# Decode step with paged indexer keys: pages loaded by register address and scored four at a time, without a gathered copy

## The chip, the cores and the metric

The kernel runs on one core of a Trainium2 chip. The metric is the device time of one execution in microseconds, and the figure shown for a kernel is the median of its timed runs. A separate execution is profiled; its trace is where all rows below come from. Names of engines: PE is the matrix engine (PEld its weight load), DVE the vector engine, ACT the scalar engine, POOL GpSimd, and SP the engine that here does nothing but issue DMAs. Each engine executes its own instructions strictly in order.

## The reference, cut to what matters

One layer of a hybrid decoder is computed for a prompt of 512 tokens and for 8 sample sequences of one token each. Both go through one projection, a gated DeltaNet in eight heads, a sparse attention, an output projection and a feed-forward of width 8192. The change touches only the sparse attention of the samples, and in it only the indexer: every sample scores all of its 4096 past keys and its own key, and keeps the best 256.

```python
def indexer_scores(q_i, w_i, k_i):
    s = jax.nn.relu(jnp.einsum("bqhd,bld->bqhl", q_i, k_i).astype(F32))
    return jnp.einsum("bqhl,bqh->bql", s, w_i.astype(F32)) * (D_IDX ** -0.5)
...
    ki_past = cache_kidx[page_table].reshape(B, past, D_IDX)
    ki_all = jnp.concatenate([ki_past.astype(k_i_new.dtype), k_i_new], axis=1)
...
    score = indexer_scores(q_i, w_i, ki_all)
    idx, valid = select_topk(score, q_pos, key_pos, n_sel)
```

There are 16 indexer heads of 128, and the past keys lie in pages of 128 keys x 128 numbers, 64 KB each in fp32. The page table names 32 pages for each of the 8 samples, so 256 pages, 16.8 MB, are read.

## The kernel before, in words

The whole layer is one stream of weight tiles through PE. All 520 tokens are the moving operand, in two halves of 260 columns; a weight tile of 128 output columns is loaded from memory in two pieces of 512 KB (line 363, tile `wr`), split by ACT and DVE into a high and a low part (lines 327 and 328), and multiplied in three products for each of 16 blocks of rows and each half (lines 446 to 448, tile `acc`). The order of the weight tiles is written out by hand (`ORDER`): indexer queries `qi0` to `qi15`, then heads of `k` and `z`, the shared keys and values, and so on. From `qi15` on, an operation of the modulation (`ada_op`, line 481) follows each tile; it takes two more pieces of 512 KB and issues four fp32 matmuls of 32 output rows by 512 columns, each on its own quarter of the array's columns (`tile_position=(0, 32*g)`).

Everything that is not this stream is a Python generator (a job) that is advanced by one step at every tick; a tick falls after each quarter of a tile and half. So the order of instructions on each engine is fixed when the kernel is built: a job's yields say how much of the stream stands between its steps. `topk` (lines 814 to 833) starts its prompt selection on POOL with three `affine_select` (line 823), which come ten ticks after `qi15`, and goes on on DVE (lines 829 and 830). `conv` (line 1295 and on) needs POOL as well (line 1302).

The sample scores are made in two steps. `gather_pages` copies all pages into a scratch tensor `kscr` in the order of the page table: 16 rounds of two halves, each an indirect DMA of 512 KB into a tile `gst` (line 856) and a plain DMA from there to `kscr` (line 858), all issued by POOL. A round is let go by a small copy of a finished accumulator (`pace`, lines 788 and 851), so that the rounds lie along the stream of `qi` tiles. `scores`, ten ticks after `qi15`, then loads four pages of one sample with one DMA of 256 KB from `kscr` (line 877, tile `pg`, issued by SP, the queue that loads the weights too), one load for each tick; up to three loads later it multiplies them by the sample's 32 query columns (two samples share a quarter of the array; line 868). So the 64 products of 32 rows x 512 columns come one at a time, each with a tick's worth of the stream between it and the next. After the eight products of a block `c` the result is rectified and reduced over the heads (lines 887 to 897). Eight blocks make the 4096 keys.

Tiles come from shared sets of buffers: `b` (24 buffers of 2 KB per partition: page tiles, convolution tiles, head tiles), `d` (4 buffers, `gst` among them), `s` (11 small ones), and four `wr` buffers. A load into a buffer waits on SP until the last reader of the buffer is done.

Of the kernel before, what the change touches and what calls it, by code (L numbers as in the profile page):

```python
# [9 lines left out]
F32 = mybir.dt.float32  # L10
F32R = mybir.dt.float32r
I32 = mybir.dt.int32
AF = mybir.ActivationFunctionType
OP = mybir.AluOpType
# [14 lines left out]
PAST = 4096  # L29
NPG = PAST // 128  # L30
# [26 lines left out]
G0 = 6  # L57
TK = (1, 2, 2)
RXB = 5
TD = 3  # L60
SY = 2
SW = 10
RXL = 4
# [174 lines left out]
class Kern:  # L238
# [541 lines left out]
    def qidx(self, j, accs):  # L780
        nc = self.nc
        if j == NE:
            self.bias_rows()
        qh, ql = self.B("qih", [128, NT], F32R), self.B("qil", [128, NT], F32R)
        self.evac(qh, accs)
        if self.pacing:
            self.pace = self.tiny.tile([128, 1], F32, name="pace0")
            nc.scalar.copy(self.pace, accs[0][:, 0:1])
        for h in range(2):
            s = slice(h * HF, (h + 1) * HF)  # L790
            nc.vector.tensor_tensor(ql[:, s], accs[h], qh[:, s].bitcast(F32), op=OP.subtract)  # L791
        for s in range(2):
            o = SEQ + 4 * s - HF
            nc.scalar.copy(self.QI[:, 4 * s:4 * s + 4, 16 * s + j], accs[1][:, o:o + 4])
        yield 2
        for i in range(1, NQ):
            w = 128 * (i + 1)
            qs = slice(128 * i, w)
            ps = self.m()
            nc.tensor.matmul(ps[:, :w], qh[:, qs], self.kih[:, :w], start=True, stop=False)  # L800
            nc.tensor.matmul(ps[:, :w], qh[:, qs], self.kil[:, :w], start=False, stop=False)
            nc.tensor.matmul(ps[:, :w], ql[:, qs], self.kih[:, :w], start=False, stop=True)
            rl = self.B("rl", [128, 512])
            nc.scalar.activation(rl[:, :w], ps[:, :w], AF.Relu)
            sc = self.sc[i]
            wcol = self.wq[:, i, j:j + 1]
            if j == 0:
                nc.vector.tensor_scalar(sc, rl[:, :w], wcol, None, op0=OP.mult)
            else:
                nc.vector.scalar_tensor_tensor(sc, rl[:, :w], wcol, sc, op0=OP.mult, op1=OP.add)  # L810
            yield 1
# [21 lines left out]
            nc.vector.tensor_scalar(self.sc[i], self.sc[i], mark, -1.0, op0=OP.is_equal, op1=OP.add)  # L833
        self.masks = True

    def gather_pages(self):

        nc, I = self.nc, self.I
        self.kscr = self.dr.tile([256, 16, 1024], F32, name="kscr")
        rows = I["ckt"].rearrange("a (g d) s -> (a g) (d s)", d=8)  # L840
        pg = self.S("pgi", [128, 2], I32)
        nc.scalar.dma_start(pg, I["pt"].rearrange("o (h p) -> p (o h)", p=128))
        ix = self.S("pgx", [128, 2, 16], I32)
        nc.gpsimd.iota(ix, pattern=[[0, 2], [1, 16]], base=0, channel_multiplier=0)
        nc.gpsimd.tensor_scalar(pg, pg, 16.0, None, op0=OP.mult)
        nc.gpsimd.tensor_tensor(ix, ix, pg[:, :, None].to_broadcast([128, 2, 16]), op=OP.add)
        for g in range(16):
            while self.pace is None:
                yield 1

            mark = nc.gpsimd.tensor_copy(self.tiny.tile([128, 1], F32, name="pace"), self.pace)
            self.pace = None
            with self.tc.issue_after(mark.ins):
                for hf in range(2):
                    t = self.L("gst", [128, 1024])
                    nc.gpsimd.indirect_dma_start(out=t, out_offset=None, in_=rows,
                                                 in_offset=bass.IndirectOffsetOnAxis(ap=ix[:, hf, g:g + 1], axis=0))
                    nc.gpsimd.dma_start(self.kscr[hf * 128:(hf + 1) * 128, g], t)
        self.pacing = False

    def scores(self):

        nc = self.nc
        todo = []

        def product():
            sp, b4, s, pg = todo.pop(0)
            nc.tensor.matmul(sp[32 * b4:32 * b4 + 32, :], self.QI[:, 4 * s + b4, :], pg.rearrange("p a b -> p (a b)"),  # L868
                             start=(s == 0), stop=(s == 1), tile_position=(0, 32 * b4))

        for c in range(PAST // 512):
            sp = None
            for b4 in range(4):
                for s in range(2):
                    pg = self.B("pg", [128, 4, 128])
                    n = (4 * s + b4) * NPG + c * 4
                    nc.sync.dma_start(pg, self.kscr[n:n + 4].rearrange("t g (d s) -> (g d) t s", s=128))
                    sp = sp or self.m()
                    todo.append((sp, b4, s, pg))
                    yield 1  # L880
                    if len(todo) > TD:
                        product()
            while todo:
                yield 1
                product()
            rl = self.B("rls", [128, 512])
            nc.scalar.activation(rl, sp, AF.Relu)
            yield 1
            ps = self.m()
            for hf in range(2):  # L890
                o = 128 - (2 * c + hf)
                nc.tensor.matmul(ps[:, 0:256], self.bs[:, o:o + 128], rl[:, hf * 256:(hf + 1) * 256],
                                 start=(hf == 0), stop=(hf == 1))
            if c == 0:
                nc.scalar.copy(self.SC[:, 0:256], ps[:, 0:256])
            else:
                nc.vector.tensor_tensor(self.SC[:, 0:256], self.SC[:, 0:256], ps[:, 0:256], op=OP.add)

        p2 = self.m()
        for b4 in range(4):  # L900
            for s in range(2):
                b = 4 * s + b4
                nc.tensor.matmul(p2[32 * b4:32 * b4 + 32, 0:1], self.QI[:, b, :], self.ki[:, SEQ + b:SEQ + b + 1],
                                 start=(s == 0), stop=(s == 1), tile_position=(0, 32 * b4))
        rn = self.S("rn", [128, 1])
        nc.scalar.activation(rn, p2[:, 0:1], AF.Relu)
        yield 2
        p2 = self.m()
        nc.tensor.matmul(p2[:, 8:9], self.bs[:, 113:241], rn, start=True, stop=True)
        nc.vector.tensor_tensor(self.SC[:, 256:257], p2[:, 8:9], self.c("cm"), op=OP.add)  # L910
        self.spawn(self.select())
# [342 lines left out]
    def stage_in(self):  # L1254
        nc, I, kp = self.nc, self.I, self.kp
# [30 lines left out]
        self.qb, self.nl, self.nkeys, self.natt = {}, {}, 0, 0  # L1286
        self.zdone, self.odone, self.sdone, self.wdone = set(), set(), set(), set()
        self.masks = self.attending = False
        self.pace, self.pacing = None, True
        self.nqb = 0  # L1290

    def conv(self, name, h, accs):
# [402 lines left out]

    def proj(self, name):
        accs = self.stream(self.x1)
        if self.pacing and not name.startswith("qi"):
            self.pace = self.tiny.tile([128, 1], F32, name="pace0")
            self.nc.scalar.copy(self.pace, accs[0][:, 0:1])  # L1700
        self.post(name, accs)

    def post(self, name, accs):
# [22 lines left out]
            self.gate(h, accs, getattr(self, "mx", None))  # L1726

    def open_in(self):
        self.kn = self.S("kn", [128, 2])
        self.rel = self.S("rel", [32, 8]), self.L("oh", [32, 640])  # L1730
        for t, n in ((self.kn, "kn"), (self.rel[0], "rel"), (self.rel[1], "oh")):
            self.nc.scalar.dma_start(t, self.I[n])
        self.stage_in()
        self.spawn(self.gather_pages())

    def open_mix(self):

# [543 lines left out]
```

## Time and profile before

| | |
|---|---|
| median of 3 timed runs | 2928.33 us (2926.22 to 2936.08) |
| the profiled execution | 2940.01 us |
| its span, first to last instruction | 2938.3 us |
| mean granted clock of PE | 0.966 of full speed |
| instructions | 55405 |
| moved by DMA | 499.64 MB, of which 37.76 MB on the queue that POOL feeds |

The span is what the rows below divide; 1.7 us of the profiled execution lie outside it.

### The profile page before, as it was taken

Reading aid. Unit: us, or ns where it says so; the run is one execution under the profiler, and the core shown is the slowest. Engines: PE = TensorE matmul, PEld = TensorE weight load, DVE = VectorE, ACT = ScalarE, POOL = GpSimd, SP = SyncE. Lnnn points to the kernel's source line nnn. Section 1 sums busy time; section 2 is a strip of 40 time slices with the busy share of each in tenths; the row PEclk is TensorE's granted clock in tenths of the full one; section 3 lists DMA queues with packets and bytes.
Section 4 is the critical chain, followed back from the end, with each engine's and each line's share of the span. In section 5 each row is a group of like instructions: output and inputs, shape, how many; then the busy total and the mean of one; then the engine's idle time right before and its main releaser. Section 6 shows DMA issues by size and latency. Waiting matters only on the chain.

```text
span 2938.3 us, 55405 instructions
## 1 busy us (share of the span) xinstructions
PE 2736.5 (93%) x21584; PEld 2508.4 (85%) x21584; DVE 1731.0 (59%) x3367; ACT 1573.6 (54%) x2796; POOL 1133.8 (39%) x961
## 2 busy tenths in 40 slices
PE   6999969999998998999988999999999898998996
PEld 3689856778897887888987999999999898898996
DVE  4464264338576555632786555555566666776767
ACT  3234222223544443333565777777778676676863
POOL 0012221112212333211463665565675556545513
PEclk9999989999999999999998999999999999999998
DMA  7868766754443555567665434334343333332354
GB/s 259 284 225 260 251 222 192 218 166 156 154 153 123 186 162 179 193 238 261 222 202 160 144 123 141 130 127 141 126 153 131 108 121 125 109 108 102 116 174 158
DMA packets 201533, 499.64 MB, mean 170 GB/s; under 512 B 23832, under 2 KB 74392, under 8 KB 201272
## 3 DMA queue, kind: packets, MB, share of 16 engines
q1 hardware_dynamic: 162544, 421.81, 43.1%
q10 hardware_dynamic: 27464, 36.53, 4.1%
q0 software_dynamic: 11264, 37.76, 3.6%
q8 instruction: 170, 2.79, 0.4%
q14 instruction: 91, 0.75, 0.1%
HBM read 430.34 MB, written 65.68 MB: 169 GB/s over the span
## 4 chain that ended last, share of the span: by engine, by line
PE 63%; DVE 10%; DMA 10%; ACT 6%; issue 5%; POOL 5%; another core or an unknown queue 0%; ACTq 0%; SPq 0%; POOLq 0%; DVEq 0%
PE acc L446 18%; PE acc L447 17%; PE acc L448 17%; DMA gst<-in_ckt,pgx 4%; ACT wh L431 3%; DVE wl L437 3%; POOL S L374 3%; PE m L868 2%; PE m L481 2%; ACT stg L436 2%; DMA kscr<-gst 2%; DVE xf L328 1%; PE m L590 1%; DMA wr<-in_win 1%; PE m L275 1%
## 5 line engine op out<-in xcount | busy, mean ns | idle before, releaser
L437 DVE TENSOR_TENSOR wl<-stg,wh 128x512 fp32r<-128x512 f32 (+1 forms) x584 | 489.7, 866 | 377.3 <-ACT wh L431 318.8
L446 PE MATMUL acc<-hh,wh 128*128 128x260 f32 (+1 forms) x1984 | 591.6, 300 | 11.7 <-DVE qil L791 6.0
L448 PE MATMUL acc<-hh,wl 128*128 128x260 f32 (+1 forms) x1984 | 567.0, 287 | 12.3 <-DVE wl L328 12.2
L447 PE MATMUL acc<-hl,wh 128*128 128x260 f32 (+1 forms) x1984 | 569.5, 287 | 0.6 <-DVE hl L623 0.6
L446 PE MATMUL acc<-xf,wh 128*128 128x260 f32 x1824 | 525.9, 288 | 42.2 <-DVE f L2164 21.9
L448 PE MATMUL acc<-xf,wl 128*128 128x260 f32 x1824 | 524.1, 287 | 6.7 <-DVE wl L328 4.8
L328 DVE TENSOR_TENSOR wl<-wr,wh 128x512 fp32r<-128x512 f32 (+1 forms) x478 | 352.1, 751 | 295.9 <-ACT wh L327 292.0
L447 PE MATMUL acc<-xf,wh 128*128 128x260 f32 x1824 | 523.3, 287 | 0.0
L327 ACT CAST wh<-wr 128x512 fp32r<-128x512 f32 (+1 forms) x478 | 284.3, 612 | 437.1 <-PE acc L447 193.9
L446 PEld LDWEIGHTS acc<-hh,wh 128*128 128x128 f32 (+1 forms) x1984 | 376.7, 190 | 113.0 <-issue 80.8
L374 POOL TENSOR_TENSOR S<-wr,wr 128x1024 f32<-128x1024 f32 x112 | 274.8, 2454 | 329.9 <-DMA wr<-in_wff 257.2
L446 PEld LDWEIGHTS acc<-xf,wh 128*128 128x128 f32 x1824 | 352.0, 193 | 45.5 <-ACT wh L431 19.2
L448 PEld LDWEIGHTS acc<-hh,wl 128*128 128x128 f32 (+1 forms) x1984 | 377.3, 190 | 14.4 <-DVE wl L328 12.6
L447 PEld LDWEIGHTS acc<-hl,wh 128*128 128x128 f32 (+1 forms) x1984 | 377.8, 190 | 8.4 <-DVE hl L623 4.8
L448 PEld LDWEIGHTS acc<-xf,wl 128*128 128x128 f32 x1824 | 352.0, 193 | 8.1 <-DVE wl L328 5.0
L447 PEld LDWEIGHTS acc<-xf,wh 128*128 128x128 f32 x1824 | 351.9, 193 | 0.0
L436 ACT COPY stg<-S 128x512 f32<-128x512 f32 (+1 forms) x334 | 241.7, 732 | 105.5 <-DVE wl L437 81.8
L448 PE MATMUL acc<-h2h,wl 128*128 128x260 f32 x928 | 266.5, 287 | 8.5 <-DVE wl L328 8.5
L446 PE MATMUL acc<-h2h,wh 128*128 128x260 f32 x928 | 266.1, 287 | 7.5 <-ACT h2h L327 5.2
L447 PE MATMUL acc<-h2l,wh 128*128 128x260 f32 x928 | 266.5, 287 | 4.5 <-DVE h2l L328 4.5
L446 PE MATMUL acc<-T,wh 128*128 128x260 f32 x896 | 256.4, 286 | 8.0 <-DVE fr L2020 3.0
L448 PE MATMUL acc<-T,wl 128*128 128x260 f32 x896 | 256.5, 286 | 2.0 <-DVE wl L328 2.0
(545 smaller groups left out, 5882.4 us busy)
## 6 DMA issues: line engine op xcount, KB each, us to landing
wr<-in_wff SPq DMA_DIRECT2D x256, 512.0 KB
wd<-in_wada SPq DMA_DIRECT2D x106, 512.0 KB
wr<-in_win SPq DMA_DIRECT2D x106, 512.0 KB
wr<-in_wada SPq DMA_DIRECT2D x86, 512.0 KB
wr<-in_wout SPq DMA_DIRECT2D x48, 512.0 KB
st<-f SPq DMA_DIRECT2D x32, 520.0 KB
kscr<-gst POOLq DMA_DIRECT2D x32, 512.0 KB
pg<-kscr SPq DMA_DIRECT2D x64, 256.0 KB
```

The source lines that it names most:

```text
L275: self.nc.tensor.transpose(out, in_, self.ident[:n, :n])
L327: self.nc.scalar.copy(hh, x)
L328: self.nc.vector.tensor_sub(hl, x, hh.bitcast(F32))
L374: self.nc.gpsimd.tensor_tensor(t, a, b, op=op)
L431: nc.scalar.copy(hh, x)
L436: nc.scalar.copy(p, x[:, s])
L437: nc.vector.tensor_tensor(hl[:, s], p, hh[:, s].bitcast(F32), op=OP.subtract)
L446: T.matmul(acc, wh[:, cs], xh, start=first, stop=False, skip_group_check=goes_on)
L447: T.matmul(acc, wh[:, cs], xl, start=False, stop=False, skip_group_check=goes_on)
L448: T.matmul(acc, wl[:, cs], xh, start=False, stop=last, skip_group_check=goes_on)
L481: self.nc.tensor.matmul(self.aacc[v][32 * g:32 * g + 32, :], self.cs[:, kt, :], w[:, j * 512:(j + 1) * 512], start=(kt == 0), stop=(kt == ...
L868: nc.tensor.matmul(sp[32 * b4:32 * b4 + 32, :], self.QI[:, 4 * s + b4, :], pg.rearrange("p a b -> p (a b)"), start=(s == 0), stop=(s == 1) ...
```

## The change

`gather_pages`, `kscr` and the pacing copies go. The page table is loaded once into one partition (`ptab`). A new method `pages(c, b)` reads four entries of it into registers of SP, and SP issues four DMAs, one for each page, 64 KB each, straight from the cache with the page's number as a register in the address; the four land in one `pg` tile as before. `scores` now asks for the pages of four samples (one call for each tick), and issues their four products one directly behind the other, one on each quarter of the array; a group is multiplied after the next group's loads have been issued. Rectifying and reducing stay as they were.

```diff
-    def gather_pages(self):
...
-        for g in range(16):
-            while self.pace is None:
-                yield 1
-
-            mark = nc.gpsimd.tensor_copy(self.tiny.tile([128, 1], F32, name="pace"), self.pace)
-            self.pace = None
-            with self.tc.issue_after(mark.ins):
-                for hf in range(2):
-                    t = self.L("gst", [128, 1024])
-                    nc.gpsimd.indirect_dma_start(out=t, out_offset=None, in_=rows,
-                                                 in_offset=bass.IndirectOffsetOnAxis(ap=ix[:, hf, g:g + 1], axis=0))
-                    nc.gpsimd.dma_start(self.kscr[hf * 128:(hf + 1) * 128, g], t)
-        self.pacing = False
+    def pages(self, c, b):
+
+        nc = self.nc
+        pg = self.B("pg", [128, 4, 128])
+        n = b * NPG + c * 4
+        rows = self.I["ckt"]
+        _, at = nc.values_load_multi_w_load_instructions(self.ptab[0:1, n:n + 4], engines=[mybir.EngineType.SP],
+                                                         min_val=0, max_val=rows.shape[0] - 1,
+                                                         skip_runtime_bounds_check_because="the DMA checks its address")
+        for t in range(4):
+            nc.sync.dma_start(pg[:, t], rows[ds(at[t], 1)].rearrange("o d s -> (o d) s"))
+        return pg
 
     def scores(self):
 
         nc = self.nc
         todo = []
+        sp = [None]
 
         def product():
-            sp, b4, s, pg = todo.pop(0)
-            nc.tensor.matmul(sp[32 * b4:32 * b4 + 32, :], self.QI[:, 4 * s + b4, :], pg.rearrange("p a b -> p (a b)"),
-                             start=(s == 0), stop=(s == 1), tile_position=(0, 32 * b4))
-
-        for c in range(PAST // 512):
-            sp = None
-            for b4 in range(4):
-                for s in range(2):
-                    pg = self.B("pg", [128, 4, 128])
-                    n = (4 * s + b4) * NPG + c * 4
-                    nc.sync.dma_start(pg, self.kscr[n:n + 4].rearrange("t g (d s) -> (g d) t s", s=128))
-                    sp = sp or self.m()
-                    todo.append((sp, b4, s, pg))
-                    yield 1
-                    if len(todo) > TD:
-                        product()
-            while todo:
-                yield 1
-                product()
+
+            c, s, pgs = todo.pop(0)
+            if s == 0:
+                sp[0] = self.m()
+            for b4, pg in enumerate(pgs):
+                nc.tensor.matmul(sp[0][32 * b4:32 * b4 + 32, :], self.QI[:, 4 * s + b4, :],
+                                 pg.rearrange("p a b -> p (a b)"), start=(s == 0), stop=(s == 1),
+                                 tile_position=(0, 32 * b4))
+            if s == 0:
+                return
             rl = self.B("rls", [128, 512])
-            nc.scalar.activation(rl, sp, AF.Relu)
+            nc.scalar.activation(rl, sp[0], AF.Relu)
             yield 1
...
+        for c in range(PAST // 512):
+            for s in range(2):
+                pgs = []
+                for b4 in range(4):
+                    pgs.append(self.pages(c, 4 * s + b4))
+                    yield 1
+                todo.append((c, s, pgs))
+                pgs = None
+                if len(todo) > 1:
+                    yield from product()
+                    yield 1
+        yield 2
+        yield from product()
...
     def open_in(self):
+        self.ptab = self.kp.tile([1, 256], I32, name="ptab")
+        self.nc.scalar.dma_start(self.ptab, self.I["pt"])
...
-        self.spawn(self.gather_pages())
```

The rest of the diff takes out the pacing copies (lines 785 to 787 and 1697 to 1700) and the constant `TD`.

## Rows read from the trace of the kernel before

**Rows 1.** The page, part 1: busy us, share of the span, instructions.
```profile
PE 2736.5 (93%) x21584; PEld 2508.4 (85%) x21584; DVE 1731.0 (59%) x3367; ACT 1573.6 (54%) x2796; POOL 1133.8 (39%) x961
```

**Rows 2.** Stretches: engines' busy us (instructions), then clock, DMA share, GB/s.
```profile
0.00:195.00 195.00, 162.43 (x1136) 113.15 (x1137) 88.26 (x225) 55.31 (x112) 9.25 (x29) 0.96 0.74 252
195.00:330.00 135.00, 133.91 (x1037) 129.43 (x1036) 69.94 (x161) 56.96 (x169) 37.34 (x52) 1.00 0.79 243
330.00:404.00 74.00, 45.54 (x330) 42.64 (x329) 27.48 (x66) 15.45 (x42) 22.23 (x36) 0.79 0.75 269
404.00:640.00 236.00, 235.97 (x1475) 164.17 (x1476) 106.18 (x304) 61.97 (x151) 40.93 (x83) 1.00 0.64 199
```

**Rows 3.** The same view in stretches of 10 us; PE's busy time stands first.
```profile
330.00:340.00 10.00, 4.58 (x35) 4.38 (x34) 1.97 (x4) 1.89 (x7) 2.94 (x5) 0.92 0.90 356
...
370.00:380.00 10.00, 3.57 (x30) 3.36 (x28) 0.00 (x0) 0.00 (x0) 4.29 (x6) 0.80 0.73 244
380.00:390.00 10.00, 2.54 (x10) 2.23 (x10) 5.72 (x14) 1.39 (x2) 3.79 (x10) 0.50 0.58 207
390.00:400.00 10.00, 0.86 (x5) 0.86 (x5) 10.00 (x27) 2.24 (x4) 0.59 (x1) 0.50 0.64 207
```

**Rows 4.** Waits of PE, DVE and POOL: us in total, times, longest.
```profile
PE acc L448 <- DVE wl L328: 11.8, 1, 11.8
PE m L275 <- DVE cu L1313: 11.3, 1, 11.3
...
DVE m L829 <- POOL sc L823: 24.6, 1, 24.6
...
POOL kscr L858 <- DMA gst<-in_ckt,pgx: 99.3, 30, 19.7
```

**Rows 5.** Timelines of POOL and ACT: start us, us, instruction, idle before it.
```profile
383.37 0.56 POOL L858 DMA_DIRECT2D kscr<-gst  x1 [1.40 <-DMA gst<-in_ckt,pgx]
383.94 0.30 POOL L823 TENSOR_SCALAR_AFFINE_SELECT sc<-sc 128x128 f32<-128x128 f32 x1
...
337.20 0.62 ACT L327 CAST wh<-wr 128x512 fp32r<-128x512 f32 x1 [10.24 <-DMA wr<-in_win]
```

**Rows 6.** The chain that ended last, 400 to 642 us, by line.
```profile
by line: PE m L868 25.4%; PE acc L446 23.6%; PE acc L447 19.0%; PE acc L448 19.0%; PE m L481 4.6%; PE m L275 3.0%; PE m L892 2.9%; PE m L1363 2.5%; PE m L903 0.1%; issue 0.0%
```

**Rows 7.** PE's timeline around one product of line 868 (two records each).
```profile
404.68 0.28 PE L448 MATMUL acc<-hh,wl 128*128 128x260 f32 x1
404.89 1.04 PE L868 MATMUL m<-pg,QI 128*32 128x512 f32 x2
...
406.09 0.28 PE L447 MATMUL acc<-hl,wh 128*128 128x260 f32 x1
```

**Rows 8.** PE's timeline around one modulation operation, four matmuls, eight records.
```profile
365.98 0.28 PE L447 MATMUL acc<-hl,wh 128*128 128x260 f32 x1
366.10 0.28 PE L448 MATMUL acc<-hh,wl 128*128 128x260 f32 x1
366.31 1.06 PE L481 MATMUL m<-wr,cs 128*32 128x512 f32 x8
...
367.53 0.29 PE L447 MATMUL acc<-hl,wh 128*128 128x260 f32 x1
```

**Rows 9.** DMA issues by line: ns min/median/max, first and last start us.
```profile
L877 SPq DMA_DIRECT2D pg<-kscr x64: 359/487/3040, 388.4 to 613.5; - x64
...
L1574 SPq DMA_DIRECT2D sst<-in_sts x8: 327/328/393, 778.2 to 1142.5; - x8
...
L856 POOL DMA_INDIRECT gst<-in_ckt,pgx x32: 933/998/1452, 195.0 to 378.0; - x32
```

**Rows 10.** DMA issues from 404 to 640 us; then a wait of SP.
```profile
wr<-in_win SPq DMA_DIRECT2D x24, 512.0 KB
wr<-in_wada SPq DMA_DIRECT2D x23, 512.0 KB
...
SPq L877 <- DMA gscr<-hkd: 12.1, 2, 6.3
```

More of the change, by code (lines that the diff above doesn't have):

```diff
@@ L59 @@
 RXB = 5
-TD = 3
 SY = 2
@@ L785, in qidx @@
         self.evac(qh, accs)
-        if self.pacing:
-            self.pace = self.tiny.tile([128, 1], F32, name="pace0")
-            nc.scalar.copy(self.pace, accs[0][:, 0:1])
         for h in range(2):
@@ L834, in topk @@
         self.masks = True
-    def gather_pages(self):
[L838 to L846, printed above, removed]
-        for g in range(16):
-            while self.pace is None:
-                yield 1
-            mark = nc.gpsimd.tensor_copy(self.tiny.tile([128, 1], F32, name="pace"), self.pace)
-            self.pace = None
-            with self.tc.issue_after(mark.ins):
-                for hf in range(2):
-                    t = self.L("gst", [128, 1024])
-                    nc.gpsimd.indirect_dma_start(out=t, out_offset=None, in_=rows,
-                                                 in_offset=bass.IndirectOffsetOnAxis(ap=ix[:, hf, g:g + 1], axis=0))
-                    nc.gpsimd.dma_start(self.kscr[hf * 128:(hf + 1) * 128, g], t)
-        self.pacing = False
+    def pages(self, c, b):
[9 more added lines that the diff above has]
+        return pg
     def scores(self):
@@ L1288, in stage_in @@
         self.masks = self.attending = False
-        self.pace, self.pacing = None, True
         self.nqb = 0
@@ L1697, in proj @@
         accs = self.stream(self.x1)
-        if self.pacing and not name.startswith("qi"):
-            self.pace = self.tiny.tile([128, 1], F32, name="pace0")
-            self.nc.scalar.copy(self.pace, accs[0][:, 0:1])
         self.post(name, accs)
```

## The prediction

> **What bounds the kernel now.** I read the page's busy times first: PE is busy 93% of the span, so a change pays only where it takes work off PE or fills one of PE's gaps [rows 1]. Then I cut the span at the places where the changed code runs. The reader is to compare PE's busy time with the length of each stretch [rows 2]. Up to 195 us PE idles 32.6 us; the change touches nothing there. From 195 to 330 us, where most of the gather runs, PE idles only 1.1 of 135 us: the gather's traffic is hidden there, and taking it away is worth at most that 1.1 us. From 330 to 404 us, where the gather ends, PE is busy 45.5 of 74 us at a clock of 0.79: this is a hole. From 404 to 640 us, the time of the score products, PE is busy without a break (235.97 of 236) at full clock: whatever leaves PE there shortens the run, as long as loads and the other engines keep up.
>
> The hole in steps of 10 us: PE idles 5.4, 6.4, 7.5 and 9.1 us in four of them, 28.4 us in all, and in two of them its granted clock is 0.50, the lower of its two levels (1.2 of 2.4 GHz); it fell while PE had nothing to do [rows 3]. The waits say why. PE waits 11.8 us for a split weight and 11.3 us for a convolution, both of DVE; DVE itself stood still 24.6 us for POOL's `affine_select` [rows 4]. On POOL that instruction started 0.01 us after the last `kscr` DMA had been issued, and that DMA had waited for its `gst` [rows 5]. So the hole is POOL's order: the selection's mask sits behind a chain of gather rounds in which POOL waited 99.3 us for `gst` tiles [rows 4]. The second PE wait is the backlog that DVE had after it. The 5.4 us at 330 us are another thing: ACT waited 10.24 us for a weight [rows 5] while the DMA engines moved 356 GB/s at a share of 0.90 [rows 3].
>
> In the products' stretch the chain of waits passes through line 868 for 25.4% of 242 us, 61.5 us [rows 6]. That is the second place to win.
>
> **Part one: no gather.** It removes 32 indirect DMAs, 32 plain DMAs and their waits on POOL, 33.5 MB of traffic (each page in and out) and 16 pairs of pacing copies on ACT and POOL, all of which lay under PE's work. The mask is then issued when its data is there, and DVE's stall and the backlog go. The worth: 28.4 us of idle PE, plus the work done at the lower clock. The stretches from 380 to 400 us hold 15 matmul records, and a few more follow; at twice 0.12 us each, with the slower restart, I estimate 3 us. Upper end 31 us. Lower end 23 us: the hole at 330 us stays, because other large copies also stand in the queues then, and 26 less a backlog of 3 us remains. Nearest to the rows is the upper end, since both waits of PE lead to the same instruction on POOL; I take 30 us.
>
> **Part two: groups of four.** A product alone costs this: from the last ordinary matmul before it to the second after it 406.09 - 404.68 = 1.41 us pass [rows 7], where ordinary ones follow at 0.12 us, so 0.24 us [rows 8]. It costs 1.17 us. Four matmuls of the very same form (32 output rows, 512 columns, fp32, one on each quarter of the array) stand in the trace at line 481: 367.53 - 366.10 = 1.43 us, so 1.19 us for all four [rows 8]. So 64 products cost 64 x 1.17 = 75 us, less some 3 us where one falls beside such a modulation group already: 72 us. Sixteen groups cost 16 x 1.19 = 19 us. Gain 53 us. Bounds: 43 us (the chain's 61.5 us less 19) and 56 us (75 less 19, nothing overlapped before). I take 53 us, because the matmul starts are what PE's next work sees.
>
> **Part three: what the shorter stretch exposes.** 236 - 53 = 183 us must now hold the same loads. 236 us at 199 GB/s are 47 MB [rows 2]; in 183 us that is 257 GB/s, at a DMA share of 0.64 x 236 / 183 = 0.83. Pieces and bytes of the page loads stay (512 rows of 512 B for a tile, as from `kscr`). What covers the loads is the lead of the queue, and less PE work now covers each. Below: nothing lost, as from 195 to 330 us, where PE was full at 243 GB/s and 0.79 [rows 2]. Above: PE idles as up to 195 us at 252 GB/s, 32.6 of 195 us or 17%, which in 183 us is 31 us [rows 2]. The demand is steady, as in the first case, but the engines are fuller than there; I take 13 us. DVE (106 us) and ACT (62 us) have room in 183 us [rows 2].
>
> **Part four: SP.** Each `pg` tile took one issue of 0.487 us median [rows 9]; now it takes a read of four registers and four issues. No row shows a register read or an address out of a register. A 128-row load issues in 0.327 us [rows 9], so 256 page issues cost at least 84 us, and at 0.487 us 125 us. SP also issues 47 weight pieces in this stretch [rows 10], about 17 us at 0.36 us each, between the two prices. So SP has (183 - 17) / 256 = 0.65 us for one page before it, and not PE, sets the pace. Between 0.327 or 0.487 and 0.65 us lie 0.16 to 0.32 us for a page's share of the register read and its address arithmetic. Lower bound of that unknown: nothing visible. Upper bound: a whole page at 0.998 us, the issue of an indirect DMA, the one row in which an address is data [rows 9]; then 256 x 0.998 + 17 = 272 us, 89 us over. A plain issue is the nearer row, being SP's own and of the same 128 rows, while the indirect one is POOL's; I take 0.6 us, so SP keeps up, barely.
>
> The Trainium skill has a price where the rows have none, and it speaks against the change: "DMA: Bandwidth & Descriptors", in Latency and other measured facts, puts the floor of a register load at about 600 ns. If the four entries come with one load, an estimate by that page is 0.15 us for a page on top of 0.33 to 0.49 us, and the sum stands; if each entry pays it, 0.93 to 1.09 us, and nearly all of the gain is gone. No run here shows it yet.
>
> **Buffers.** Page tiles in flight go from about 4 to 8 or 12 of the 24 shared buffers. SP already stood 12.1 us in two waits for a buffer that another tile's store still read, 6.3 us the longest [rows 10]. In the sum it is hidden behind SP's other waiting; without that cover it is a rival.
>
> **Sum.** 30 + 53 - 13 = 70 us. The profiled execution of 2940.0 us would become 2870 us. The median of the runs shown is 11.7 us lower, and nothing in these stretches explains that difference, so I take the 70 us off the median: 2858 us. The likeliest case's own range: most 31 + 56 - 0 = 87, least 23 + 43 - 31 = 35, so 2841 to 2893 us.
>
> **The rivals.**
>
> (A) The forecast, PE still sets the pace: 2858 us, chance 0.50.
>
> (B) SP sets the pace of the score stretch, mildly: a page costs 0.65 to 0.97 us. For: one page's known cost already uses half to three quarters of its time, and SP is in order, so a weight's load stands behind the register reads. Against: 64 x 0.487 and 17 us of issuing make 48 of 236 us, so SP now mostly waits for free buffers. At 0.8 us: 256 x 0.8 + 17 = 222 us, 39 us over 183; the gain is 83 - 39 = 44 us, 2884 us. Chance 0.20.
>
> (C) The other side: the same place, but a page costs more than 0.97 us, which is where the stretch is 83 us longer than 183 us and the whole gain is eaten: (266 - 17) / 256. At the indirect issue's 0.998 us the gain is 83 - 89 = -6 us, 2934 us; with 0.15 us more for the register read it is 256 x 1.15 + 17 = 311 us, 45 us slower, 2973 us. For: four register reads in a row with nothing of SP's own to hide them. Against: plain issues at a third of that. Chance 0.15, of which 0.05 within 0.3%.
>
> (D) SP waits for page buffers: at one wait of 6.3 us in each of the eight blocks, a weight is late by 50 us in all, of which the 13 us are already in the sum: 70 - 37 = 33 us, 2895 us. For: the two waits of the present trace. Against: after the products four buffers come free at once. Chance 0.08.
>
> (E) The groups are issued together but don't run together, since the four stationary tiles differ where line 481 has one and the same: then part two gives nothing and part three costs nothing, 30 us, 2898 us. Against: each matmul of line 481 is a matmul with its own weight load in the code too. Chance 0.04.
>
> (F) The hole closes only in part, because the mask then waits for DVE's own scores: 20 us of part one stay, 2878 us. Chance 0.03.
>
> **How the numbers follow.** 0.3% of 2928 us, 9 us, is about what a measurement of this kernel can tell from no change. A, B, D, E and F are faster: 0.85; within 0.3%: 0.05; slower: 0.10. The range must leave out no more than 2 in 10: from 2838 us, just under A's best, up to 2925 us, which takes in B, D, E and F and leaves out C and the edge of A.
>
> **What the profile would show.** Part one right: no wait of DVE for line 823 above 2 us, and PE full at clock 1.00 between 330 and 400 us. Part two right: 16 groups of eight records of the product's line, each in about 1.06 us. Part three: the stretch of the products at about 195 us, DMA at 240 to 260 GB/s, PE's waits there on ACT's `wh` and weights. Part four: SP's register reads with their time, and SP waiting for buffers again; in B or C it would never wait, and issue without a break while PE waits for `pg` and `wr`. The prediction is wrong if a page costs SP more than 0.65 us.

## The result, and the profile after

The changed kernel takes 2891.92 us (median of 4 runs, 2890.65 to 2892.96) against 2929.32 us of the kernel before, run in turn with it: a ratio of 0.9869, interval 0.9851 to 0.9887. It is 37.4 us faster, about half of the 70 us that the sum gave, and at the slow edge of the likeliest case's own range (2841 to 2893 us). Its profiled execution has a span of 2888.9 us at a mean clock of 0.972.

The page, part 1, of the kernel after, for [rows 1]:

```profile
PE 2696.3 (93%) x21584; PEld 2498.0 (86%) x21584; DVE 1736.6 (60%) x3367; ACT 1573.7 (54%) x2780; POOL 1072.0 (37%) x878
```

The same number of matmuls now keeps PE busy 40.2 us less. Stretches of the kernel after, columns as in [rows 2]:

```profile
195.00:330.00 135.00, 134.20 (x1044) 130.03 (x1043) 70.09 (x154) 57.59 (x156) 0.00 (x0) 1.00 0.39 95
330.00:404.00 74.00, 71.05 (x549) 62.11 (x551) 59.63 (x168) 20.98 (x51) 10.14 (x23) 1.00 0.49 154
374.00:574.00 200.00, 184.36 (x1297) 144.21 (x1296) 95.11 (x268) 53.08 (x136) 38.19 (x79) 0.98 0.68 213
...
330.00:340.00 10.00, 10.00 (x82) 9.86 (x81) 3.41 (x6) 2.84 (x7) 0.00 (x0) 1.00 0.32 107
...
380.00:390.00 10.00, 7.62 (x56) 6.14 (x56) 9.87 (x28) 2.31 (x5) 3.72 (x9) 1.00 0.49 153
390.00:400.00 10.00, 9.91 (x71) 7.93 (x70) 10.00 (x31) 2.98 (x7) 1.71 (x3) 1.00 0.39 111
```

From 195 to 330 us PE is as full as before while DMA traffic fell from 243 to 95 GB/s: that gather was hidden, as the prediction said. The hole is shut: PE is busy 71.05 of 74 us from 330 to 404 us, where it was 45.54, and the clock stays at 1.00, so 25.5 us of idle are gone. DVE's longest waits after, from 330 to 410 us, where [rows 4] had 24.6 us for POOL:

```profile
DVE sc L806 <- ACT rl L800: 5.2, 2, 4.0
DVE wl L327 <- ACT wh L326: 4.7, 4, 1.8
```

POOL is no longer among them. The products now run from 374 to 574 us, 200 us instead of 236, but PE is no longer full there: it idles 15.6 us.

Issues and products of the kernel after, columns as in [rows 9]:

```profile
L838 SPq TENSOR_LOAD <-ptab x64: 293/301/675, 357.3 to 567.6; - x64
L842 SPq FUSED_REGOPS  x256: 37/37/51, 357.9 to 569.5; - x128
L842 SPq MOVE pg<-in_ckt x256: 29/29/37, 358.0 to 569.6; - x128
L842 SPq DMA_DIRECT2D pg<-in_ckt x256: 332/333/1308, 358.1 to 569.6; - x128
```

One register load fetches the addresses of four pages in 0.301 us; each page then takes two short register instructions and an issue of 0.333 us. SP's timeline after shows what that comes to with the gaps between instructions (start us, us, line, count):

```profile
372.53 0.86 SPq L362 DMA_DIRECT2D wr<-in_win  x2
373.98 25.56 SPq L842 DMA_DIRECT2D pg<-in_ckt  x36
399.64 0.38 SPq L362 DMA_DIRECT2D wr<-in_wada  x1
400.55 7.86 SPq L842 DMA_DIRECT2D pg<-in_ckt  x12
...
428.26 0.38 SPq L362 DMA_DIRECT2D wr<-in_win  x1
429.16 9.57 SPq L842 DMA_DIRECT2D pg<-in_ckt  x16
```

Sixteen pages take 9.57 us, 0.60 us for a page: the price that the prediction took. All 256 are 154 us of SP's time; with 17 us for weights that is 171 us in a stretch of 200. From 374.0 to 399.6 us SP issues 36 pages and not one weight. The waits after, from 370 to 600 us, show who pays:

```profile
ACT wh L326 <- DMA wr<-in_win: 99.0, 20, 11.7
...
SPq L362 <- DMA wr<-in_win: 17.8, 5, 5.9
SPq L842 <- DMA gscr<-hkd: 3.2, 2, 2.3
SPq L362 <- PE m L480: 1.2, 1, 1.2
```

ACT, which splits each weight, stands 99.0 us waiting for weights to land. SP waits only 1.2 us for a buffer that PE still holds; in an experiment below, where the loads are cheap, that wait is 49.3 us. Such a wait is SP being ahead: here the lead is gone. The wait of [rows 10] for a page buffer is now 3.2 us.

PE's timeline after, around the products of three tiles (records, two to a product):

```profile
374.41 1.06 PE L857 MATMUL m<-pg,QI 128*32 128x512 f32 x6
375.40 0.39 PE L445 MATMUL acc<-hh,wh 128*128 128x260 f32 x1
...
380.87 0.59 PE L857 MATMUL m<-pg,QI 128*32 128x512 f32 x1 [1.35 <-DMA pg<-in_ckt]
380.88 0.62 PE L480 MATMUL m<-wr,cs 128*32 128x512 f32 x2
...
403.74 1.07 PE L857 MATMUL m<-pg,QI 128*32 128x512 f32 x8
```

At 403.74 us a whole group of four takes 1.07 us, as line 481 did in [rows 8]. At 374.41 us only three of a group stand together; the fourth product runs apart from them at 380.87 us, beside a modulation, after PE waited 1.35 us for its page. By the trace seven of the 16 groups stand whole and by themselves, and two more run mixed with the four matmuls of a modulation. Six have fallen into three and one, and one into a pair and two single products. A single product takes a slot of its own, of about 1.05 us. Since the order of instructions on PE is fixed when the kernel is built, which groups are broken is part of the program and not of one execution.

### The profile page after: what moved, and what is told of

Same layout as the page of the kernel before. It is cut to its first block, busy times and chain, and to the rows that moved or that the text cites. A ratio compares the mean times of both kernels' runs of the same rounds, so it can differ in the third digit from the quotient of the medians.

```text
span 2888.9 us, 56203 instructions
## 1 busy us (share of the span) xinstructions
PE 2696.3 (93%) x21584; PEld 2498.0 (86%) x21584; DVE 1736.6 (60%) x3367; ACT 1573.7 (54%) x2780; POOL 1072.0 (37%) x878
```

## The experiments

Ratios and gains are against the kernel before, timed together with each experiment. Its own median was 2929.3 us beside the changed kernel and 2934.5 to 2939.4 us beside the experiments, so ratios are what is to be compared. Each edit is cut to its main lines and shown against the changed kernel; that of part one alone is shown against the kernel before.

**Part one alone.** Pages by register address; the product loop of the kernel before.

```diff
+                    pg = self.pages(c, 4 * s + b4)
-                    pg = self.B("pg", [128, 4, 128])
-                    n = (4 * s + b4) * NPG + c * 4
-                    nc.sync.dma_start(pg, self.kscr[n:n + 4].rearrange("t g (d s) -> (g d) t s", s=128))
```

> Half of the change: no gather, pages by register address, but the products one at a time as before. Theories: (SP) in the changed kernel a page costs SP 0.60 us in order, so weights and pages come late in the score stretch and eat the gain of the groups; (split) the groups of four fall apart on PE, 8 of 16 stay whole, and that eats it; (DMA) the engines are too full in the shorter stretch. All three expect the hole at 330 to 400 us to close, 35 us, so 2894 us. (SP) adds that 172 us of issuing lie under a stretch of 236 us, so nothing more is lost, and this kernel is within 10 us of the changed one.

Measured: 2913.69 us, 0.9909 (0.9886 to 0.9931), 25.1 us faster. Its products run from 371.9 to 606.9 us with PE full:

```profile
372.00:607.00 235.00, 234.75 (x1439) 161.76 (x1438) 104.72 (x296) 58.27 (x147) 41.95 (x82) 1.00 0.64 200
```

With 235 us to issue the same 256 page loads in, PE idles 0.3 us: SP's time costs it nothing there. The hole's closing is worth what the lower part of the predicted 23 to 31 us said, and 10 us less than was expected here.

**Part two alone.** The gather and `kscr` stay; groups of four, one 256 KB load for a tile.

```diff
...
+        self.nc.sync.dma_start(pg, self.kscr[n:n + 4].rearrange("t g (d s) -> (g d) t s", s=128))
-        for t in range(4):
-            nc.sync.dma_start(pg[:, t], rows[ds(at[t], 1)].rearrange("o d s -> (o d) s"))
```

> The other half: gather and scratch copy as before, one load of 256 KB for a tile, products in groups of four. (SP): SP has 1 issue in place of 4 and a register read, so the stretch loses most of 53 us: 2880 to 2890 us. (split): the order on PE has 15 groups whole, so the same. (DMA): bytes and pieces are those of the changed kernel, so only some 8 us come of it: 2921 us. The hole before the stretch stays in all.

Measured: 2889.36 us, 0.9831 (0.9812 to 0.985), 49.4 us faster. The stretch of its products, and then a wait of DVE between 300 and 420 us:

```profile
412.00:580.00 168.00, 164.87 (x1292) 137.48 (x1294) 93.69 (x262) 55.06 (x138) 38.73 (x76) 1.00 0.82 259
```

```profile
DVE m L829 <- POOL sc L823: 21.5, 1, 21.5
```

The hole is still there (DVE's wait of 21.5 us for the mask), the groups pay in full, and the shorter stretch exposes only 3.1 us although DMA runs at 259 GB/s and a share of 0.82. Part three's 13 us were too many.

**Both parts with loads that cost SP next to nothing.** One load of four neighbouring pages at a fixed address for each tile.

```diff
+        nc.sync.dma_start(pg, rows[n:n + 4].rearrange("t d s -> d t s"))
...
-        for t in range(4):
-            nc.sync.dma_start(pg[:, t], rows[ds(at[t], 1)].rearrange("o d s -> (o d) s"))
```

> The changed kernel with one load of 256 KB from four neighbouring pages at a fixed address in place of the register read and four loads; it scores other pages than the page table names, so its output is not the reference's; bytes and pieces are the same. (SP): both gains come, 35 + 40 to 53 us: 2841 to 2855 us. (split): only the 8 to 10 us of broken groups come back: 2882 us. (DMA): as the changed kernel, 2892 us.

Measured: 2863.52 us, 0.9749 (0.9728 to 0.9769), 75.2 us faster: the sum of the two parts alone (25.1 + 49.4 = 74.5). Its stretch, then its page issues, then two waits from 370 to 600 us:

```profile
375.00:544.00 169.00, 165.48 (x1296) 137.50 (x1294) 95.04 (x270) 55.46 (x139) 39.39 (x77) 1.00 0.82 258
```

```profile
L838 SPq DMA_DIRECT2D pg<-in_ckt x64: 367/467/2060, 358.2 to 531.0; - x64
```

```profile
ACT wh L326 <- DMA wr<-in_win: 64.7, 18, 9.6
SPq L362 <- PE m L480: 49.3, 11, 6.7
```

The same pages' worth of bytes and the same matmuls fit into 169 us. So neither the traffic nor the groups take the changed kernel's missing 37 us; the way in which its pages are issued does.

**Is it the broken groups?** The last-loaded tile's product goes first and the other three behind it.

```diff
...
+            last = one(3)
+            with self.tc.issue_after(last.ins):
+                for b4 in range(3):
+                    one(b4)
-            for b4, pg in enumerate(pgs):
...
```

> The changed kernel with the product of the last loaded tile issued first and the other three queued behind it, so that 14 groups stay whole on PE and two fall into pairs; SP's work is unchanged. (SP): at most 7 us come back, since a whole group then waits for its last page: 2885 to 2895 us. (split): 10 to 20 us come back: 2872 to 2882 us. (DMA): 2892 us.

Measured: 2896.92 us, 0.9863 (0.9842 to 0.9884), no different from the change. By its trace 12 of its 16 groups stand whole, three run mixed with a modulation's four, and one falls into two pairs; and it gains nothing. The stretch of its products:

```profile
381.00:575.00 194.00, 176.14 (x1261) 141.63 (x1261) 89.52 (x251) 51.32 (x133) 37.25 (x78) 0.96 0.67 210
```

PE's groups by line there (busy us and mean ns, then idle us before them and what ended most of it):

```profile
L857 PE MATMUL m<-pg,QI 128*32 128x512 f32 x128 | 23.8, 633 | 2.8 <-DMA pg<-in_ckt 2.8
L480 PE MATMUL m<-wr,cs 128*32 128x512 f32 x72 | 16.7, 603 | 6.9 <-DMA wr<-in_wada 6.9
```

The same groups of the kernel after, from 374 to 574 us:

```profile
L857 PE MATMUL m<-pg,QI 128*32 128x512 f32 x128 | 29.1, 601 | 1.4 <-DMA pg<-in_ckt 1.3
...
L480 PE MATMUL m<-wr,cs 128*32 128x512 f32 x80 | 18.6, 602 | 5.0 <-DMA wr<-in_wada 5.0
```

The products take 5.3 us less of PE, but PE now idles 194 - 176.14 = 17.9 us in the stretch where it idled 15.6, more of it for pages and modulation weights. This stretch begins 7 us later than the other; from 372 to 600 us, which holds both, PE idles 23.8 us here and 19.7 us in the kernel after. Whole groups alone win back nothing that can be measured: the loads are as late as before.

**Is it the register addresses, or the number of loads?** Four loads at fixed addresses for each tile, no register.

```diff
...
+            nc.sync.dma_start(pg[:, t], rows[n + t:n + t + 1].rearrange("o d s -> (o d) s"))
-            nc.sync.dma_start(pg[:, t], rows[ds(at[t], 1)].rearrange("o d s -> (o d) s"))
```

> The changed kernel with four loads of 64 KB for a tile, but at fixed addresses: no register is read, no address worked out (it scores other pages, so its output is not the reference's). Two theories of what on SP is dear: (R) the register read and the address, 0.35 us for a tile and 0.13 us for a page, 0.87 of a tile's 2.42 us; (N) the number of DMAs, 256 in place of 64, each 0.33 us of SP in order, and 38 us more in all than 64 issues. (R) expects most of the gain back, 65 to 75 us below the kernel before; (N) expects little, 40 to 50 us below.

Measured: 2886.01 us, 0.9832 (0.9803 to 0.986), 53.4 us faster, between the two. Its issues:

```profile
L839 SPq DMA_DIRECT2D pg<-in_ckt x256: 327/430/1509, 357.0 to 556.1; - x128
```

256 x 0.43 = 110 us of SP's time cost some 24 us against 30 us of it (64 x 0.467) in the kernel with one fixed load for a tile. These two sums leave out the gaps between issues; with them 16 fixed page loads take 7.55 us on SP's timeline, 0.47 us each or 121 us in all, against the change's 0.60 us. A fixed issue held SP for 0.43 us at the median, not for the 0.33 us that (N) took. Register work is a part of the price, not all of it.

**Few loads, but as much of SP's time.** One 256 KB load for a tile, its address the sum of five single register loads; it loads other pages than the reference's.

```diff
...
+        k = (at[0] + at[1] + at[2] + at[3] + at[4]) // 8
+        nc.sync.dma_start(pg, rows[ds(k, 4)].rearrange("t d s -> d t s"))
-        for t in range(4):
-            nc.sync.dma_start(pg[:, t], rows[ds(at[t], 1)].rearrange("o d s -> (o d) s"))
```

> As the kernel with one fixed load of 256 KB for a tile, but with five register reads and their sum ahead of it, so that SP is held about 2.3 us for a tile (2.4 in the changed kernel) with 64 DMAs in place of 256; it scores other pages, so its output is not the reference's. If SP's time alone is what costs: 38 to 45 us below the kernel before. If the number of DMAs costs, or the places that the weights' loads have between them on SP: 65 to 75 us below.

Measured: 2902.22 us, 0.9884 (0.9864 to 0.9904), 32.3 us faster: as little as the change. Its stretch, then four tiles on SP's timeline, then its register loads:

```profile
379.00:597.00 218.00, 179.87 (x1294) 147.66 (x1293) 99.31 (x287) 55.14 (x139) 37.62 (x77) 0.90 0.64 204
```

```profile
403.58 7.41 SPq L847 DMA_DIRECT2D pg<-in_ckt  x4
```

```profile
L841 SPq TENSOR_LOAD <-ptab x320: 262/272/952, 361.9 to 587.1; - x160
```

Four issues end 7.41 us after the first began, so one tile holds SP (7.41 - 0.37) / 3 = 2.35 us, four pages' worth of the change (4 x 0.60 = 2.4 us). It has 64 loads, the large pieces and 15 whole groups of the fast kernel, and loses the same. So SP's time is enough to cause the loss, without small loads and without broken groups; with the fixed loads above, which lose 24 us without a register, neither the number and size of the DMAs nor the register address as such is needed for it. Where PE waits differs, though. Two waits from 370 to 600 us:

```profile
ACT wh L326 <- DMA wr<-in_win: 103.3, 17, 17.6
PE m L873 <- ACT rls L868: 23.0, 4, 9.5
```

ACT again stands waiting for weights, as in the change (99.0 us). Here PE's largest wait is for the rectified scores, which ACT makes in its own order, behind the weights that it has to split. PE's granted clock fell as well (0.90 over the stretch against 1.00), and PE was busy 179.9 us with nearly the same matmuls that took it 165.5 us in the kernel with one fixed load for a tile.

**Other engines issue the pages.** All of them POOL, then all of them ACT.

```diff
...
+            nc.gpsimd.dma_start(pg[:, t], rows[ds(at[t], 1)].rearrange("o d s -> (o d) s"))
-            nc.sync.dma_start(pg[:, t], rows[ds(at[t], 1)].rearrange("o d s -> (o d) s"))
```

> The changed kernel with the register read and the four loads of a tile issued by POOL in place of SP; all is computed. SP is free of pages. (SP) expects the full gain, 70 to 80 us below the kernel before, if POOL's issues don't hold up its convolution work. A rival on POOL: 256 issues at the 0.56 us of its plain DMAs before are 143 us of a stretch of 190, POOL's convolution steps come late and 30 us are lost: 45 us below.

Measured: 2915.07 us, 0.993 (0.9903 to 0.9957), 24.3 us faster: less than either theory expected.

> The same issued by ACT, which also splits the weights. (SP) as a theory of an in-order issuer: 155 us of issuing and 62 us of ACT's work do not fit a stretch of 190 us, so the weights' high parts come late: slower than the changed kernel, 0 to 30 us below the kernel before. If what costs is not the issuer's time but the number of small loads in flight, it is as the changed kernel, 38 us below.

Measured: 2921.27 us, 0.9946 (0.993 to 0.9962), 18.1 us faster, as the first theory expected. The first kernel's issues and a wait of PE:

```profile
L842 POOL DMA_DIRECT2D pg<-in_ckt x256: 534/534/796, 360.6 to 600.3; - x128
```

```profile
PE m L857 <- DMA pg<-in_ckt: 17.9, 8, 4.2
```

The second kernel's issues and two waits from 350 to 620 us:

```profile
L842 ACTq DMA_DIRECT2D pg<-in_ckt x256: 339/340/1517, 354.3 to 607.9; - x128
```

```profile
DVE wl L327 <- ACT wh L326: 78.7, 14, 20.2
ACT cx L1287 <- DMA pg<-in_ckt: 54.4, 4, 19.4
```

On POOL a page costs more and the products themselves come late (17.9 us of PE's waiting for pages). On ACT the computation that stands behind a page load on the same engine waits (54.4 us), and with it the weights' splitting. Moving the whole work moves the queue.

**Half of the pages on POOL, half on SP; then a quarter.** Everything is computed.

```diff
+        eng, q = ((mybir.EngineType.SP, nc.sync), (mybir.EngineType.Pool, nc.gpsimd))[b % 2]
...
+            q.dma_start(pg[:, t], rows[ds(at[t], 1)].rearrange("o d s -> (o d) s"))
-            nc.sync.dma_start(pg[:, t], rows[ds(at[t], 1)].rearrange("o d s -> (o d) s"))
```

(For the quarter: `[b % 4 == 3]`.)

> The changed kernel with the tiles of every second sample issued by POOL and the others by SP, register reads included; all is computed. (SP): 78 us of issuing on SP and some 70 to 90 us on POOL both fit under 190 us: 65 to 80 us below the kernel before, the best of the kernels that compute everything. If small loads themselves cost, as the changed kernel, 38 us below.

Measured: 2873.10 us, 0.9789 (0.9763 to 0.9816), 66.3 us faster.

> The tiles of every fourth sample issued by POOL, the others by SP; all is computed. If the loss goes with the time that SP spends on pages (155 us in the changed kernel, 116 us here, 78 us with half on POOL): between the two, 50 to 58 us below the kernel before. If the number of small loads in flight costs: as the changed kernel, 38 to 42 us.

Measured: 2884.41 us, 0.9824 (0.9801 to 0.9846), 50.1 us faster. The stretch of the half, then its issues, then two waits from 370 to 600 us:

```profile
373.00:555.00 182.00, 170.32 (x1292) 140.33 (x1293) 96.35 (x271) 56.37 (x141) 101.81 (x199) 0.98 0.76 239
```

```profile
L843 SPq DMA_DIRECT2D pg<-in_ckt x128: 332/333/1513, 356.5 to 541.4; - x128
L843 POOL DMA_DIRECT2D pg<-in_ckt x128: 537/537/798, 357.8 to 550.0; - x128
```

```profile
ACT wh L326 <- DMA wr<-in_win: 60.5, 16, 9.2
SPq L362 <- PE m L480: 33.4, 9, 6.7
```

SP has its lead back (33.4 us of waiting for a buffer) and ACT's waiting for weights is down from 99.0 to 60.5 us. The half has the best median of the versions that compute everything, and its interval lies clear of the change's. All but one of its groups stand whole, as in the kernel with one fixed load for a tile, so two things are better at once here: SP's time and the order on PE. The kernel with the last product first shows that mending most of the order alone does not bring this. POOL's pages go through a queue of their own in other packets (3840 for 7.87 MB), but at the same DMA time for a byte: from 373 to 555 us 13.9% of the engines' time for those 7.87 MB, 52.7% for the 29.38 MB of SP's queue.

**Pages queued behind the latest weight.** Alone, and with the half on POOL.

```diff
+            self.lastw = self.nc.sync.dma_start(t, ap)
-            self.nc.sync.dma_start(t, ap)
...
+        with self.tc.issue_after(self.lastw.ins):
```

> The changed kernel with each tile's loads queued behind the latest weight load that stands before them in the program, so that SP's order no longer has nine tiles in a row ahead of a weight; the work on SP is the same. If late weights by SP's order cost: 50 to 60 us below the kernel before. If SP's time costs wherever the weights stand: 38 to 42 us below.

Measured: 2897.55 us, 0.9872 (0.9851 to 0.9892), 37.0 us faster.

> The tiles of every second sample issued by POOL, and SP's loads behind the weights as in the kernel with the weights first; all is computed. If both help: 70 to 75 us below the kernel before, better than the half on POOL alone (66). If the order doesn't matter once SP has room: 66 us.

Measured: 2876.97 us, 0.9804 (0.9782 to 0.9826), 57.5 us faster. Neither differs from its parent, and SP's timeline of the first says why it proves little:

```profile
373.81 25.41 SPq L843 DMA_DIRECT2D pg<-in_ckt  x36
399.32 0.38 SPq L362 DMA_DIRECT2D wr<-in_wada  x1
```

The same 36 pages still run without a weight between them. The edit hardly changed SP's order, so what another order would give stays open.

**All together.** For each kernel: SP's time on page loads (pages or tiles by their time); for the stretch of the products PE's idle time, the busy time of the products' line and of the modulation's line 480, and how much the sum of these three exceeds that of the cheap fixed loads (33.2 us); last the loss against that kernel by the ratios, (ratio - 0.9749) x 2935 us. Each ratio's interval is 0.002 to 0.003 wide on either side, some 6 to 8 us.

| pages issued | SP on pages, us | idle + products + modulation, us | excess | loss by the ratio |
|---|---|---|---|---|
| one fixed load a tile | 64 x 0.467 = 30 | 3.5 + 18.1 + 11.6 | 0 | 0 |
| half by POOL | 128 x 0.60 = 77 | 11.7 + 20.3 + 10.6 | 9.4 | 11.7 |
| quarter by POOL | 192 x 0.60 = 115 | 17.0 + 21.2 + 13.7 | 18.7 | 22.0 |
| four fixed loads a tile | 256 x 0.43 = 110 | 8.5 + 28.3 + 17.9 | 21.5 | 24.4 |
| the change | 256 x 0.60 = 154 | 15.6 + 29.1 + 18.6 | 30.1 | 35.2 |
| one held load a tile | 64 x 2.35 = 150 | 38.1 + 19.7 + 12.5 | 37.1 | 39.6 |

The loss rises with SP's time: from 0.25 us for each further us of it (11.7 for 77 - 30) to 0.33 (39.6 for 150 - 30). The first step is not clear of noise: the interval of the half (from 0.9763) still meets that of the cheap fixed loads (to 0.9769). With the gaps between its issues, 121 us, the row of four fixed loads stands in order as well. The loss appears as single products, as the modulation's own groups, which break as well, or as plain waiting, and most of each loss is found in this one stretch. In the kernel with one held load for a tile it is nearly all waiting, and the other work at the lower clock comes on top of the excess shown.

SP's time is not the whole measure, though. In part one alone the same 154 us of pages, (154 + 17) / 235 = 73% of the stretch, left PE idle for 0.3 us; with a quarter on POOL (115 + 17) / 192 = 69% of the stretch cost about 22 us.

## Why the prediction came out as it did

**Part one** held: the mask no longer waits, DVE's longest wait there is 4.0 us, and 25.5 us of idle and the clock came back. Measured alone 25.1 us, for 30 taken. The 5.4 us at 330 us, which the lower end kept, went too; a new gap of 2.4 us stands at 380 to 390 us.

**Part two** held in size: the groups alone bring 49.4 us, and a whole group takes 1.07 us. The sign that was named, sixteen groups of eight records, did not appear: seven stand so, and two more are mixed with a modulation's four.

**Part three** was too large: 3.1 to 3.5 us of idle instead of 13, at 258 GB/s and 0.82, the traffic that was forecast. Without SP's term the sum would have been near 75 us, which the cheap loads show.

**Part four is the step that failed**: "So SP has (183 - 17) / 256 = 0.65 us for one page before it, and not PE, sets the pace", and from that "I take 0.6 us, so SP keeps up, barely", a cost of nothing. The price was right to the second digit (0.60 us), which is luck, since no row gave it and it was picked between 0.33 and 1.00 us; the threshold was wrong. At 0.60 us SP would be busy 171 of 183 us, and the sum treated that as free. With products in groups the runs show no such point: 77 us of SP's time already cost about 12 us, which is not quite clear of noise, 115 us cost 22, and 154 us cost 35 of the 75. SP issues in order, so a weight stands behind whatever pages precede it, and its lead over PE (49.3 us of waiting with cheap loads, 33.4 with half, 1.2 in the change) shrinks with that time. That the lost lead is what costs is argued: SP's wait for PE does not order the losses, as 12.2 us of it are left where one held load a tile loses 39.6 us. Taken at 0, this term measured about 35 us. With part three's 10 us back and part one 5 us smaller, 70 - 35 + 10 - 5 = 40 us, against 37.4 us measured.

The sign that was named for being wrong, a page above 0.65 us, did not come either: it watched SP's price and not what SP's time costs below saturation. Of the rivals B is nearest: the loss is SP's, but at a price that the prediction had put on A's side, and SP never became the busy queue without a wait that B named; it still waits 17.8 us before loading weights. C did not come: no page costs 0.97 us. One register load, 0.301 us, serves four pages. The Trainium skill, "DMA: Bandwidth & Descriptors", Latency and other measured facts, gives about 600 ns as its floor; this trace does not agree, with 0.301 us for one load of four entries, and the measurement decides. D is out: 3.2 us of waiting for page buffers. E is out: 1.07 us for four. F is out: no wait of DVE for POOL remains at the hole's place.

What stays open: why SP's time costs a quarter to a third of itself well below saturation, and why it cost nothing when the products came one at a time. The run of 36 pages without a weight speaks for bursts, but the attempt to put weights between them did not change the order, so bursts are argued and not shown. That the fixed loads read other pages than the reference's may also matter a little; their bytes and pieces are the same.

## What to carry to other kernels

Do not put an in-order issuing queue's new duty at nothing because the queue stays under 100% busy: look for its waits for free buffers before the change, and when the new duty eats them, expect loss in whatever else that queue loads. When one load becomes four with an address each, share the issuing between two queues that have room, and test that split before the whole move. If four matmuls must run together, count whole groups in the trace after, but ask first what came late before mending the groups.

## What the runs showed of the hardware

- A register load costs nearly the same for one entry as for four: 0.272 us and 0.301 us on SP; four take 0.317 us on ACT and 0.319 us on POOL. An address out of a register adds 0.066 us of register instructions to a page's issue, which then takes 0.333 us at the median; the same load at a fixed address, one behind the other, takes 0.430 us (least 0.327 us).
- The same 64 KB issue with a register address takes 0.333 us on SP, 0.340 us on ACT and 0.534 us on POOL.
- Four matmuls of 32 output rows with four different stationary tiles take 1.07 us together, about as long as four with one and the same, 1.06 us [rows 8].
- With cheap loads PE stayed at clock 1.00 and idled 3.5 of 169 us under 258 GB/s at a share of 0.82; loads with a lead were hidden there.
